# A hybrid decoder block on one core: queries and keys split before their way through DRAM, the identity loaded later, fewer idle products at the start

## The chip, the cores and the metric

The kernel runs on one core of a Trainium2 chip. The metric is the device time of one launch in microseconds; the time quoted is the median of three runs. Beside it stands one profiled execution, whose span runs from the first to the last instruction of the core.

## What is computed

One layer of a decoder block over 512 tokens of width 1024, in float32. The part that the change touches is the attention of the middle stage:

```python
h = h + 0.5 * swiglu(rmsnorm(h, norm_ffn1[i]), ffn1_w1[i], ffn1_w3[i], ffn1_w2[i])
z = rmsnorm(h, norm_mix[i]) @ w_in[i]
q, kc, vc, ksl, vsl, kw, vw, g, u = jnp.split(z, split_at, axis=-1)
...
q = rope(q.reshape(B, L, N_HEADS, HEAD_DIM), pos)
kc = rope(kc.reshape(kvshape), pos)
ksl = rope(ksl.reshape(kvshape), pos)
...
s = jnp.einsum('bqghd,bsgd->bghqs', qc, k_w).astype(jnp.float32) * scale
p_win = masked_softmax(s, wmask)
o_win = jnp.einsum('bghqs,bsgd->bqghd', p_win.astype(v_w.dtype), v_w)
```

There are 8 query heads of width 64, two key heads, and three branches: compressed, selected and window keys. Beside the attention runs a diagonal state space mixer (S5); after both come the output projection, a second SwiGLU, a gated per-layer embedding and a last norm.

## The kernel before

**Products in three parts.** A float32 operand is split in a high part, rounded to the type that TensorE takes in one pass (FR), and the low remainder. A product is the sum of three: high by high, high by low, low by high (`mm3`). The high part is made by ScalarE (a copy or a scaled activation), the low part by VectorE (a subtraction). Weights come from DRAM in units of 128 x 1024 (`load_unit`, L114; split in L159 and L160), through a ring of four raw buffers and three split ones, on SyncE's queue.

**Stages.** By the trace: the first feed-forward network to about 375 us, the mixer to 603 us, the second network to about 975 us, the gate and the last norm to the end. Activations lie transposed, 128 rows of the model by 512 tokens, in eight tiles `h`.

**The start.** SyncE loads the first weight unit in halves, the eight tiles of `h` and three more units. GpSimd loads the identity (L126), makes a bfloat16 copy of it (`identb`, L128) and fills `ones` (L130). TensorE multiplies `ones` by `ones` `WARM` times into a bank that nobody reads (L134, `ps_D<-ones`); each such product in full float32 shows as two records. The real first products, `ps_A` and then `ps_B`, take `xh` (L181, ScalarE) and `xl` (L182, VectorE), which are `h` scaled by the norm's gain and split. The squares for the norm are L187 and L191 (ScalarE) and L192 (VectorE).

**The mixer's queries and keys.** `rotary` (L963) turns two projections: four products and two sums on VectorE give the two rotated halves, which go to DRAM unsplit (L974, L975): keys to `kd`, queries to `qd`. Rows return in another order, so that a head's 64 numbers lie on 64 partitions. For keys, four blocks `kf` are loaded twice (L983, L984), ScalarE makes `KA` (high, in both halves of the partitions) and VectorE makes `KB` (low, in the lower half). For queries, `scores` (L1130) loads for each of the four blocks of 128 tokens two tiles `qf`, twice each (L1142, L1143); ScalarE scales and rounds into `QA` and `QB` (L1144, L1145), VectorE puts the low part into the upper half of `QA` (L1146), and ScalarE clears the upper half of `QB` (L1148).

**The scores.** For each group of heads, TensorE multiplies `QA` by `KA`, `QB` by `KB` and adds the mask (`ps_B` and `ps_C`, two banks each); VectorE takes the row maxima (L1165), ScalarE the exponentials with their sums (L1168). Only then is the bank free. Into the same stretch fall the gated unit of S5 (`glu`, L1093 to L1109) and the compressed keys (L1043 and the products from `raw`).

**What sets the order.** The order of instructions on each engine is written out: `ENGINE_ORDER` holds for each engine the steps from one traced instruction to the next, `TILE_ORDER` pairs of instructions of which the second follows the first, and `impose` turns both into dependencies. An engine runs its list strictly in that order; SyncE's list is the order in which its DMAs are issued.

Of the kernel before, what the change touches and what calls it, by code (L numbers as in the profile page):

```python
# [10 lines left out]
F32 = mybir.dt.float32  # L11
FR = mybir.dt.float32r
BF = mybir.dt.bfloat16
I32 = mybir.dt.int32
AF = mybir.ActivationFunctionType
OP = mybir.AluOpType
# [3 lines left out]
SEQ = 512  # L20
# [56 lines left out]
def block_kernel(ctx: ExitStack, tc: tile.TileContext, a: dict, out: bass.AP):  # L77
    nc = tc.nc
# [47 lines left out]
    nc.gpsimd.dma_start(ident, a["ident"])  # L126
# [669 lines left out]
    qd = dram.tile([2, 128, 2, SEQ], F32, tag="qd", name="qd")  # L796
    kd = dram.tile([128, 2, SEQ], F32, tag="kd", name="kd")
# [3 lines left out]
    def mixer(ctx):  # L801
# [161 lines left out]
        def rotary(dst, tag):  # L963
            oa = proj(tag)
            yield
            ob = proj(tag)
            a1, b1, a2, b2 = (tp.tile([128, SEQ], F32, tag=n, name=n) for n in ("r1", "rb1", "r2", "r3"))
            V.tensor_tensor(a1, oa, cosr, OP.mult)
            V.tensor_tensor(a2, oa, sinr, OP.mult)
            V.tensor_tensor(b1, ob, sinr, OP.mult)  # L970
            V.tensor_tensor(b2, ob, cosr, OP.mult)
            V.tensor_tensor(a1, a1, b1, OP.subtract)
            V.tensor_tensor(a2, a2, b2, OP.add)
            nc.sync.dma_start(dst[:, 0], a1)  # L974
            nc.sync.dma_start(dst[:, 1], a2)  # L975
            yield

        def kq():
            yield from rotary(kd, "A")
            for b in range(4):  # L980
                kf = mp.tile([128, SEQ], F32, tag="ra", name="kf", bufs=2)
                src = kd[32 * b:32 * b + 32].rearrange("r a t -> (r a) t")
                nc.sync.dma_start(kf[0:64], src)  # L983
                nc.sync.dma_start(kf[64:128], src)  # L984
                S.copy(KA[:, b], kf)
                V.tensor_tensor(KB[0:64, b], kf[0:64], KA[0:64, b].bitcast(F32), OP.subtract)
            yield from rotary(qd[0], "B")
# [142 lines left out]
        def scores(qb, env, pool, tags="B", stage=("ra", "ra")):  # L1130
# [5 lines left out]
            for i, (hs, st) in enumerate(zip((slice(0, 4), slice(4, 8)), stage)):  # L1136
                src = qd[i].rearrange("(h r) a t -> (r a) h t", h=4)[:, :, tq]
                if st == "ra":
                    qf = mp.tile([128, 4, 128], F32, tag=st, name="qf", bufs=2)
                else:  # L1140
                    qf = tp.tile([128, 4, 128], F32, tag=st, name="qf")
                nc.sync.dma_start(qf[0:64], src)  # L1142
                nc.sync.dma_start(qf[64:128], src)  # L1143
                S.activation(QA[:, hs], qf, AF.Copy, scale=0.125)  # L1144
                S.activation(QB[0:64, hs], qf[0:64], AF.Copy, scale=0.125)  # L1145
                V.scalar_tensor_tensor(QA[64:128, hs], qf[64:128], 0.125, QA[64:128, hs].bitcast(F32),  # L1146
                                       OP.mult, OP.subtract)
            S.copy(QB[64:128].rearrange("p h q -> p (h q)"), zero[64:128, 0:1].to_broadcast([64, 1024]))  # L1148
# [126 lines left out]
        def chain(*gs):  # L1275
            for g in gs:
                yield from g
# [17 lines left out]
        envs = {qb: {} for qb in range(4)}  # L1295
        s5g, pg, cg, gg = s5_all(), chain(kq(), rotary(qd[1], "B"), cmp_kv(), v_gates()), cmp_all(), glu()
        s3, s2 = scores(3, envs[3], mp, TS, G3), scores(2, envs[2], mp, TS2, G2)
# [106 lines left out]
    with tc.tile_pool(name="gate", bufs=2, reuse_waits="tile") as gp:  # L1404
# [72 lines left out]
G3 = "r1", "r2"  # L1477
G2 = "r3", "ra"
TW, TY, TP, TS, TS2 = "C", "D", "D", "B", "BC"
PROJ = 12  # L1480
WARM = 32
# [351 lines left out]
```

## Time and profile before

| | us |
|---|---|
| median of 3 runs | 1046.07 (1045.25 to 1046.2) |
| the profiled execution | 1045.7 |
| its span | 1043.9 |
| TensorE, share of the span | 98% |
| VectorE, share of the span | 78% |
| ScalarE, share of the span | 51% |

The time lies 1.8 us above the span in the profiled execution. A busy TensorE says little by itself, since the ends of its products are modelled and overlap; what counts is the distance between the starts of its products, and who is named in the chain of work that ended last.

### The profile page before, as it was taken

The page shows a single profiled execution, that of the slowest core. Times are in us where ns is not written, and L with a number is a line of the kernel's source. Part 1 is how long each engine was busy: PE and PEld are TensorE (multiplying, and loading weights), DVE is VectorE, ACT ScalarE, POOL GpSimd, SP SyncE. Part 2 cuts the span into 40 slices and gives each one's busy share as a digit, 9 for nine tenths or more (in the row PEclk, how much of TensorE's full clock was granted, in tenths as well). Part 3 has the DMA queues.
Part 4 walks back from the last instruction along what each step waited for, and adds up shares of the span by engine and source line. Part 5 has one row for each costly group of instructions (what it writes and reads, how often), then busy time and mean ns, then how long its engine had stood idle before and what let it go on. Part 6 is the DMA issues. An engine that isn't in the chain of part 4 may idle for free.

```text
span 1043.9 us, 16750 instructions
## 1 busy us (share of the span) xinstructions
PE 1023.4 (98%) x6386; PEld 897.8 (86%) x6386; DVE 813.1 (78%) x1357; ACT 533.8 (51%) x933; POOL 76.3 (7%) x99
## 2 busy tenths in 40 slices
PE   9999999999999999999999999999999999999995
PEld 8888899889989888896577677998999899899885
DVE  6999997778887777999798988884576477467676
ACT  6354265345425531349879846663354255155453
POOL 1000011001001010000000001101011011000000
PEclk9999999999999999999999999999999999999998
DMA  8536375756745739753710064457265545534222
GB/s 307 111 81 176 73 186 163 226 136 151 206 116 154 271 109 201 241 169 101 242 61 1 21 202 142 119 134 202 61 152 153 150 108 127 169 99 125 89 74 82
DMA packets 73121, 148.52 MB, mean 142 GB/s; under 512 B 19520, under 2 KB 30784, under 8 KB 72784
## 3 DMA queue, kind: packets, MB, share of 16 engines
q1 hardware_dynamic: 60624, 127.05, 39.0%
q0 software_dynamic: 11552, 20.22, 11.9%
q8 instruction: 50, 0.82, 0.3%
q14 instruction: 31, 0.25, 0.1%
q10 hardware_dynamic: 864, 0.17, 0.1%
HBM read 121.96 MB, written 15.73 MB: 132 GB/s over the span
## 4 chain that ended last, share of the span: by engine, by line
PE 94%; DVE 2%; ACT 2%; issue 1%; POOL 0%; DVEq 0%; POOLq 0%; ACTq 0%
PE ps_C L134 28%; PE ps_B L134 25%; PE ps_A L134 24%; PE ps_D L134 16%; ACT ps_B L1168 1%; DVE nmax L1165 1%; PE ps_C L685 0%; DVE lo L160 0%; ACT QB L1148 0%; DVE xn L283 0%; PE ps_D L938 0%; DVE cs L1043 0%; ACT QB L1145 0%; ACT hi L159 0%; ACT QA L1144 0%
## 5 line engine op out<-in xcount | busy, mean ns | idle before, releaser
L159 ACT CAST hi<-raw 128x1024 fp32r<-128x1024 f32 (+2 forms) x206 | 212.4, 1043 | 254.4 <-PE ps_C L134 103.6
L160 DVE TENSOR_TENSOR lo<-raw,hi 128x1024 fp32r<-128x1024 f32 (+2 forms) x206 | 246.7, 1211 | 49.2 <-ACT hi L159 48.6
L134 PE MATMUL ps_C<-hq,hi 128*128 128x512 f32 x704 | 218.5, 391 | 0.0
L134 PEld LDWEIGHTS ps_C<-hq,hi 128*128 128x128 f32 x704 | 127.1, 188 | 23.0 <-issue 0.6
L134 PE MATMUL ps_C<-hq,lo 128*128 128x512 f32 x352 | 137.3, 390 | 0.0
L134 PE MATMUL ps_A<-xh,hi 128*128 128x256 f32 (+1 forms) x432 | 135.0, 313 | 0.0
L134 PE MATMUL ps_A<-xh,lo 128*128 128x256 f32 (+1 forms) x432 | 134.1, 310 | 0.0
L134 PE MATMUL ps_A<-xl,hi 128*128 128x256 f32 (+1 forms) x432 | 134.0, 310 | 0.0
L134 PEld LDWEIGHTS ps_A<-xh,hi 128*128 128x128 f32 x432 | 81.5, 189 | 5.8 <-issue 0.7
L134 PE MATMUL ps_B<-sh,hi 128*128 128x256 f32 x304 | 86.5, 285 | 0.0
L134 PEld LDWEIGHTS ps_A<-xl,hi 128*128 128x128 f32 x432 | 81.6, 189 | 5.7 <-issue 0.5
L134 PE MATMUL ps_B<-sh,lo 128*128 128x256 f32 x304 | 85.3, 281 | 0.5 <-DVE lo L160 0.5
L134 PEld LDWEIGHTS ps_A<-xh,lo 128*128 128x128 f32 x432 | 81.6, 189 | 4.6 <-DVE lo L160 0.2
L134 PE MATMUL ps_B<-sl,hi 128*128 128x256 f32 x304 | 85.4, 281 | 0.0
L487 DVE SCALAR_TENSOR_TENSOR h<-ps_C,h 128x512 f32<-128x512 f32 x64 | 44.1, 689 | 48.4 <-PE ps_C L134 48.3
L134 PEld LDWEIGHTS ps_C<-hq,lo 128*128 128x128 f32 x352 | 66.1, 188 | 14.5 <-DVE lo L160 0.3
L134 PE MATMUL ps_D<-sl,hi 128*128 128x256 f32 x236 | 66.4, 281 | 0.6 <-DVE sl L302 0.6
L134 PE MATMUL ps_D<-sh,lo 128*128 128x256 f32 x236 | 66.4, 281 | 0.0
L134 PE MATMUL ps_D<-sh,hi 128*128 128x256 f32 x236 | 66.3, 281 | 0.0
L363 POOL DMA_DIRECT2D raw<-in_wpack x38 | 35.5, 933 | 412.9 <-DMA raw<-in_wpack 309.2
L369 POOL DMA_DIRECT2D raw<-raw x38 | 32.8, 864 | 391.3 <-DVE lo L160 383.9
L134 PEld LDWEIGHTS ps_B<-sh,hi 128*128 128x128 f32 x304 | 57.2, 188 | 1.0 <-issue 0.2
(405 smaller groups left out, 2328.0 us busy)
## 6 DMA issues: line engine op xcount, KB each, us to landing
raw<-in_wpack SPq DMA_DIRECT2D x171, 512.0 KB, 4.2
raw<-in_wpack POOLq DMA_DIRECT2D x38, 256.0 KB, 4.8
raw<-raw POOLq DMA_DIRECT2D x38, 256.0 KB, 3.3
so<-s5o SPq DMA_DIRECT2D x8, 512.0 KB, 5.4
h<-in_xT SPq DMA_DIRECT2D x8, 256.0 KB, 5.1
s5f<-fs SPq DMA_DIRECT2D x4, 512.0 KB, 3.3
s5o<-gt SPq DMA_DIRECT2D x4, 512.0 KB, 3.7
s5t<-tcs SPq DMA_DIRECT2D x2, 1024.0 KB, 5.8
```

What stands on the lines that cost most here:

```text
L134: return PE.matmul(o, lhsT, rhs, start=start, stop=stop, **kw)
L159: S.copy(hi[:, c], raw[:, c])
L160: V.tensor_tensor(lo[:, c], raw[:, c], hi[:, c].bitcast(F32), OP.subtract)
L363: nc.gpsimd.dma_start(a0[:, 1], src[:, 0:512], accum_op=OP.add)
L369: nc.gpsimd.dma_start(a1[:, 1], a0[:, 1], accum_op=OP.add)
L487: V.scalar_tensor_tensor(h[:, m, :], o, 0.5, h[:, m, :], OP.mult, OP.add)
L1165: V.tensor_reduce(mc, s_, AX.X, OP.max, negate=True)
L1168: S.activation(s_[:, i, r], s_[:, i, r], AF.Exp, bias=mc[:, i, r:r + 1], accum_out=dc[:, i, r:r + 1])
```

## The change

1. `rotary` takes a scale and splits each rotated half before its way through DRAM: ScalarE makes the high part `rh` (L976), VectorE the low part in place, and each is written with a DMA of its own (L977, L980). `qd` and `kd` hold both parts.
2. `KA` and `KB` are loaded ready from `kd` with three DMAs (L986); the copies and subtractions on `kf` go.
3. `QA` and `QB` are loaded ready from `qd` with three DMAs for each block of tokens (L1138); the two activations, the activation for `QB`, the subtraction and the clearing on ScalarE go. GpSimd clears the upper half of `QB` instead (L1136).
4. The identity is loaded on SyncE's queue, at a later place.
5. 20 idle products in place of 32.
6. The tables of orders are new for all engines and through the whole program.

```diff
-    nc.gpsimd.dma_start(ident, a["ident"])
+    nc.sync.dma_start(ident, a["ident"])
...
-    qd = dram.tile([2, 128, 2, SEQ], F32, tag="qd", name="qd")
-    kd = dram.tile([128, 2, SEQ], F32, tag="kd", name="kd")
+    qd = dram.tile([2, 256, 2, SEQ], F32, tag="qd", name="qd")
+    kd = dram.tile([2, 128, 2, SEQ], F32, tag="kd", name="kd")
...
-        def rotary(dst, tag):
+        def rotary(dst, tag, scale):
...
-            nc.sync.dma_start(dst[:, 0], a1)
-            nc.sync.dma_start(dst[:, 1], a2)
+            for i, t in enumerate((a1, a2)):
+                hi = mp.tile([128, SEQ], FR, tag="ra", name="rh", bufs=2)
+                S.activation(hi, t, AF.Copy, scale=scale)
+                nc.sync.dma_start(dst[0, :, i], hi.bitcast(F32))
+                lo = t.bitcast(FR)
+                V.scalar_tensor_tensor(lo, t, scale, hi.bitcast(F32), OP.mult, OP.subtract)
+                nc.sync.dma_start(dst[1, :, i], t)
...
-            yield from rotary(kd, "A")
-            for b in range(4):
-                kf = mp.tile([128, SEQ], F32, tag="ra", name="kf", bufs=2)
-                src = kd[32 * b:32 * b + 32].rearrange("r a t -> (r a) t")
-                nc.sync.dma_start(kf[0:64], src)
-                nc.sync.dma_start(kf[64:128], src)
-                S.copy(KA[:, b], kf)
-                V.tensor_tensor(KB[0:64, b], kf[0:64], KA[0:64, b].bitcast(F32), OP.subtract)
-            yield from rotary(qd[0], "B")
+            yield from rotary(kd, "A", 1.0)
+            for part, dst in ((0, KA[0:64]), (0, KA[64:128]), (1, KB[0:64])):
+                nc.sync.dma_start(dst.bitcast(F32), kd[part].rearrange("(b r) a t -> (r a) b t", b=4))
+            yield from rotary(qd[:, 0:128], "B", 0.125)
...
-            for i, (hs, st) in enumerate(zip((slice(0, 4), slice(4, 8)), stage)):
...
-                nc.sync.dma_start(qf[0:64], src)
-                nc.sync.dma_start(qf[64:128], src)
-                S.activation(QA[:, hs], qf, AF.Copy, scale=0.125)
-                S.activation(QB[0:64, hs], qf[0:64], AF.Copy, scale=0.125)
-                V.scalar_tensor_tensor(QA[64:128, hs], qf[64:128], 0.125, QA[64:128, hs].bitcast(F32),
-                                       OP.mult, OP.subtract)
-            S.copy(QB[64:128].rearrange("p h q -> p (h q)"), zero[64:128, 0:1].to_broadcast([64, 1024]))
+            G.memset(QB[64:128].rearrange("p h q -> p (h q)").bitcast(F32), 0.0)
+            for part, dst in ((0, QA[0:64]), (0, QB[0:64]), (1, QA[64:128])):
+                nc.sync.dma_start(dst.bitcast(F32), qd[part].rearrange("(h r) a t -> (r a) h t", h=8)[:, :, tq])
...
-WARM = 32
+WARM = 20
...
-        "21:23 54 -55:7 48:3 -51:2 49:32 37:3 -40:12 49:3 -52:4 24:3 21:6 -27:9 53:3 -83 26:3 53:3 -41:3 38:3 "
+        "21:14 51 -52 51:9 -60 59:14 -73:2 71:2 -73:2 71:19 28:3 -31:3 28:3 18:3 -52:4 48:9 -30:9 21:3 -51 79:6 "
```

**The start, TensorE.** Before, the idle products `ps_D<-ones` stand thus among the first products of the first weight unit:

```order
L134 MATMUL ps_D<-ones 128x128 x23
L134 MATMUL ps_A<-xh,hi 128x512
L134 MATMUL ps_D<-ones 128x128 x7
L134 MATMUL ps_A<-xl,hi 128x512
L134 MATMUL ps_A<-xh,lo 128x512
```

Now:

```order
L134 MATMUL ps_D<-ones 128x128 x14
L134 MATMUL ps_A<-xh,hi 128x512
L134 MATMUL ps_D<-ones 128x128
L134 MATMUL ps_A<-xl,hi 128x512
L134 MATMUL ps_A<-xh,lo 128x512
```

Ahead of the second real product stand 15 idle ones where 30 stood. Of the other five, one stands between later products of `ps_A`, two ahead of the first product of `ps_B` and two before its third.

**The start, ScalarE.** Behind the split of the first half of weight unit 0, before (`acc` and `xn` are squares for the norm):

```order
L159 CAST hi<-raw 128x512
L187 ACTIVATE acc<-h 128x512
L181 ACTIVATE xh<-h,gains 128x512
L191 ACTIVATE xn<-h 128x512
L181 ACTIVATE xh<-h,gains 128x512 x5
L159 CAST hi<-raw 128x512
L181 ACTIVATE xh<-h,gains 128x512
L191 ACTIVATE xn<-h 128x512
L181 ACTIVATE xh<-h,gains 128x512
L159 CAST hi<-raw 128x1024
```

and now:

```order
L159 CAST hi<-raw 128x512
L181 ACTIVATE xh<-h,gains 128x512 x3
L159 CAST hi<-raw 128x512
L181 ACTIVATE xh<-h,gains 128x512 x5
L187 ACTIVATE acc<-h 128x512
L191 ACTIVATE xn<-h 128x512
L159 CAST hi<-raw 128x1024
```

The squares have moved behind all eight `xh`, and the second half of weight unit 0 is split after three of them instead of after six. VectorE's list has moved in the same way: all eight `xl` and the low part of that half stand ahead of the first sum of squares.

**The first scores, ScalarE.** Where the scores of the last two blocks of tokens begin, beside the gated unit (`gt`, `oh`, `sg`), before:

```order
L857 ACTIVATE gt<-gt 128x512
L1144 ACTIVATE QA<-qf 128x512
L1145 ACTIVATE QB<-qf 64x512
L1093 CAST oh<-yt 128x512
L1144 ACTIVATE QA<-qf 128x512 x2
L1148 CAST QB<-zero 64x1024
L1145 ACTIVATE QB<-qf 64x512
L1106 ACTIVATE sg<-ps_A,bglu 128x512
L1168 ACTIVATE ps_B,den<-ps_B,nmax 128x512 x2
L1145 ACTIVATE QB<-qf 64x512
L1144 ACTIVATE QA<-qf 128x512
L1145 ACTIVATE QB<-qf 64x512
```

and now, where the exponentials stand in L1158:

```order
L855 ACTIVATE gt<-yt 128x512
L1158 ACTIVATE ps_B,den<-ps_B,nmax 128x512
L1158 ACTIVATE ps_C,den<-ps_C,nmax 128x384
L857 ACTIVATE gt<-gt 128x512
L1158 ACTIVATE ps_C,den<-ps_C,nmax 128x384
L1093 CAST oh<-yt 128x512
L1158 ACTIVATE ps_B,den<-ps_B,nmax 128x512
L1106 ACTIVATE sg<-ps_A,bglu 128x512
L1158 ACTIVATE ps_B,den<-ps_B,nmax 128x512
```

No query is prepared here any more, and the first exponentials come ahead of the gated unit's last steps instead of behind them.

**The way through DRAM, SyncE.** The queue where the last rotated queries (`qd<-r`) leave, before:

```order
L974 DMA qd<-r_4578 128x512
L114 DMA raw<-in_wpack 128x1024
L901 DMA so<-s5o 128x1024 x2
L1000 DMA kcd<-ra 64x512
L1142 DMA qf<-qd 64x4x128
L975 DMA qd<-r_4580 128x512
L1143 DMA qf<-qd 64x4x128
```

and now, with the high parts in `rh`:

```order
L980 DMA qd<-r_4565 128x512
L977 DMA qd<-rh 128x512
L114 DMA raw<-in_wpack 128x1024
L901 DMA so<-s5o 128x1024
L980 DMA qd<-r_4567 128x512
L1138 DMA QB<-qd 64x8x128 x2
L1000 DMA kcd<-ra 64x512 x2
L114 DMA raw<-in_wpack 128x1024
L1138 DMA QA<-qd 64x8x128
```

There are two writes for each rotated half, and the loads of queries stand behind the last of them, since one load now takes all eight heads.

More of the change, by code (lines that the diff above doesn't have):

```diff
@@ L1128, in mixer, with scores @@
         den = mp.tile([128, 4, 3, 8], F32, name="den")
-        def scores(qb, env, pool, tags="B", stage=("ra", "ra")):
+        def scores(qb, env, pool, tags="B"):
             nk = (qb + 1) * 128
@@ L1135, in scores @@
             QB = pool.tile([128, 8, 128], FR, tag="QB", name="QB", bufs=2)
-            for i, (hs, st) in enumerate(zip((slice(0, 4), slice(4, 8)), stage)):
[L1137 to L1141, printed above, removed]
-                nc.sync.dma_start(qf[0:64], src)
-                nc.sync.dma_start(qf[64:128], src)
-                S.activation(QA[:, hs], qf, AF.Copy, scale=0.125)
-                S.activation(QB[0:64, hs], qf[0:64], AF.Copy, scale=0.125)
-                V.scalar_tensor_tensor(QA[64:128, hs], qf[64:128], 0.125, QA[64:128, hs].bitcast(F32),
-                                       OP.mult, OP.subtract)
-            S.copy(QB[64:128].rearrange("p h q -> p (h q)"), zero[64:128, 0:1].to_broadcast([64, 1024]))
+            G.memset(QB[64:128].rearrange("p h q -> p (h q)").bitcast(F32), 0.0)
+            for part, dst in ((0, QA[0:64]), (0, QB[0:64]), (1, QA[64:128])):
+                nc.sync.dma_start(dst.bitcast(F32), qd[part].rearrange("(h r) a t -> (r a) h t", h=8)[:, :, tq])
             env.update(QA=QA, QB=QB)
@@ L1295, in mixer @@
         envs = {qb: {} for qb in range(4)}
-        s5g, pg, cg, gg = s5_all(), chain(kq(), rotary(qd[1], "B"), cmp_kv(), v_gates()), cmp_all(), glu()
-        s3, s2 = scores(3, envs[3], mp, TS, G3), scores(2, envs[2], mp, TS2, G2)
+        s5g, pg, cg, gg = s5_all(), chain(kq(), rotary(qd[:, 128:256], "B", 0.125), cmp_kv(), v_gates()), cmp_all(), glu()
+        s3, s2 = scores(3, envs[3], mp, TS), scores(2, envs[2], mp, TS2)
         drain(s5_input())
@@ L1476 @@
 ORDER = 3, 2
-G3 = "r1", "r2"
-G2 = "r3", "ra"
 TW, TY, TP, TS, TS2 = "C", "D", "D", "B", "BC"
 PROJ = 12
-WARM = 32
+WARM = 20
 S1 = 32
```

320 rows, old and new, of tables (ENGINE_ORDER, TILE_ORDER) are left out of this document.

## The prediction

> **What bounds the kernel now.** First the page: the busy times and the chain that ended last.
>
> ```profile
> PE 1023.4 (98%) x6386; PEld 897.8 (86%) x6386; DVE 813.1 (78%) x1357; ACT 533.8 (51%) x933; POOL 76.3 (7%) x99
> PE 94%; DVE 2%; ACT 2%; issue 1%; POOL 0%; DVEq 0%; POOLq 0%; ACTq 0%
> ```
>
> TensorE carries 94% of the chain, so most of the program can only shrink by fewer products, and the change removes none but idle ones. What can go is the 6% on other engines (some 60 us) and the useless products at the start. So I asked next where these lie: busy times by stretch (columns PE, PEld, DVE, ACT, POOL, granted clock, DMA share, GB/s), and the chain inside the stretch of the scores.
>
> ```profile
> 400.00:476.00 76.00, 75.34 (x495) 65.14 (x494) 72.04 (x155) 29.08 (x51) 0.00 (x0) 1.00 0.71 203
> 476.00:524.00 48.00, 44.97 (x252) 28.85 (x251) 40.78 (x73) 42.85 (x104) 0.00 (x0) 1.00 0.56 166
> 524.00:603.00 79.00, 78.73 (x375) 58.62 (x374) 73.86 (x160) 68.90 (x172) 0.00 (x0) 1.00 0.09 30
> ...
> 477.69:497.33 19.64, 18.16 (x86) 11.71 (x84) 18.75 (x32) 18.44 (x44) 0.00 (x0) 1.00 0.23 68
> 497.33:516.00 18.67, 17.12 (x108) 9.46 (x108) 13.59 (x24) 16.72 (x43) 0.00 (x0) 1.00 0.83 251
> ...
> by line: PE ps_A L134 17.8%; ACT ps_B L1168 17.6%; DVE nmax L1165 14.4%; PE ps_B L134 12.7%; issue 6.3%; ACT QB L1148 5.2%; DVE cs L1043 4.5%; ACT QB L1145 4.2%; ACT QA L1144 3.9%; ACT sg L1106 3.2%; DVE ol L1109 3.0%; ACT ps_C L1168 2.5%;
> PEld ps_B L134 <- ACT ps_B L1168: 4.9, 9, 1.2
> ```
>
> From 476 to 524 us ScalarE is busy for 42.85 of 48 us, and weight loading for 28.85, the lowest of the three mixer stretches in share. The fourth and fifth rows cut the dense part of it in two. The last two rows are the chain of the 40 us from 476 to 516, and the longest wait of TensorE in the stretch: it waits nine times for an exponential before it may reuse a bank. TensorE holds little more than 30% of this piece of the chain; the scores are paced by maximum and exponential on VectorE and ScalarE, and between them, on the chain, stand the three lines that the change deletes: 5.2 + 4.2 + 3.9 = 13.3% of 40 us, which is **5.3 us**.
>
> The start, from the order of time (start, length, then what):
>
> ```profile
> 2.37 7.34 PE L134 MATMUL ps_D<-ones 128*128 128x128 f32 x46 [2.37 <-POOL ones L130]
> 9.46 0.48 PE L134 MATMUL ps_A<-xh,hi 128*128 128x512 f32 x1
> 9.78 1.72 PE L134 MATMUL ps_D<-ones 128*128 128x128 f32 x14
> ...
> 16.82 0.39 PE L134 MATMUL ps_A<-xh,lo 128*128 128x512 f32 x1
> 17.05 0.39 PE L134 MATMUL ps_B<-xh,hi 128*128 128x512 f32 x1
> ...
> 1.32 0.77 POOL L126 DMA_DIRECT2D ident<-in_ident  x1 [0.37 <-issue]
> 6.00 0.29 POOL L128 CAST identb<-ident 128x128 bf16<-128x128 f32 x1 [3.67 <-DMA ident<-in_ident]
> 6.17 0.63 ACT L191 ACTIVATE xn<-h 128x512 f32<-128x512 f32 x1 [0.69 <-DMA h<-in_xT]
> 12.36 1.03 ACT L159 CAST hi<-raw 128x1024 fp32r<-128x1024 f32 x1
> 13.95 1.22 DVE L160 TENSOR_TENSOR lo<-raw,hi 128x1024 fp32r<-128x1024 f32 x1
> ```
>
> Products of 512 columns start 0.23 us apart (16.82 to 17.05). All 24 of `ps_A` are issued by 17.05; laid end to end they would have begun at 17.05 - 24 x 0.227 = 11.6 us. This "dense start" is the measure of the head: what it gains is how much earlier the dense start lies.
>
> **The change part by part: the start.** What the first products wait for:
>
> ```profile
> L119 SPq DMA_DIRECT2D h<-in_xT x8: 421/432/631, 1.2 to 5.2; - x8
> L181 ACT ACTIVATE xh<-h,gains x8: 707/714/725, 4.8 to 11.7; 128x512 fp32r<-128x512 f32 x8
> L182 DVE SCALAR_TENSOR_TENSOR xl<-h,gains,xh x8: 747/748/749, 7.4 to 12.7; 128x512 fp32r<-128x512 f32 x8
> ...
> DMA to landing us min/median/max: 3.0/5.1/5.6
> ...
> L114 SPq DMA_DIRECT2D raw<-in_wpack x1: 328/328/328, 6.2 to 6.2; - x1
> ...
> DMA to landing us min/median/max: 5.9/5.9/5.9
> ```
>
> The first tile of `h` lands at 1.2 + 3.0 = 4.2 us, the last at 5.2 + 5.6 = 10.8, weight unit 1 at 6.2 + 5.9 = 12.1. ScalarE waits for the second tile until 6.17, so 1.9 us lie between tiles one and two, and (10.8 - 6.15) / 7 = 0.66 us between the seven pieces of the same size behind. In the wide gap the identity lands (`identb` waits for it until 6.00). Moved behind, it frees between 0 and 1.9 - 0.66 = 1.2 us; I take the middle, 0.6.
>
> Step by step: last tile of `h` at 10.2; its `xh` 0.71 later, 10.9; VectorE makes eight `xl` (8 x 0.748) and a half of `lo` (0.69) from about 5.5, so the last `xl` is there at 12.1, and `ps_A` ends near 12.6. TensorE itself: 14 idle products are 28 records, 19 slow and 9 fast by the next two rows, so they end at 2.37 + 4.10 + 9 x 0.103 = 7.4, and 24 products with two idle ones fill the time to 13.3. Unit 1 is there at 11.5, ScalarE comes to it behind `acc` and `xn` (2 x 0.63) at 12.4 and is done at 13.4; VectorE's `lo`, 1.22, at 14.65. Then stands the third product of `ps_B`, with 26 behind it, and from there nothing waits. Dense start 14.65 - 26 x 0.227 = 8.75. Gain 11.6 - 8.75 = **2.9 us**. If the identity frees nothing, all is 0.6 later, 2.3; if it frees all, 3.5. The cover of what has moved: the squares now end on ScalarE near 10.9 + 8 x 0.63 + 2 x 1.05 = 18 us, and the first norm needs them only after the two weight units, 48 products or 10.9 us, that stand between. The identity lands near 16 us (an estimate: 5.2 MB of loads ahead of it at the 384 GB/s of the second row below, from 2.4 us); GpSimd's `identb` waits for it and, behind it on GpSimd, the first norm's power, whose squares are later still. Without that cover the cost is the lateness itself.
>
> ```profile
> 2.37:6.47 4.10, 4.10 (x19) 4.10 (x20) 0.69 (x1) 2.24 (x5) 0.29 (x1) 1.00 0.94 322
> 6.47:9.46 2.99, 2.99 (x29) 2.99 (x29) 2.62 (x5) 2.92 (x5) 0.00 (x0) 1.00 1.04 384
> ```
>
> These are the idle products: 19 records in the first 4.10 us (0.216 each), 29 in the next 2.99 (0.103). The array runs at half pace until 6.47. The Trainium skill, "TensorE: Matmul & The Clock Gate", Part 1 (the HAM clock gate), says that the clock is released by about 3.4 us of sustained activity in a window that runs freely, so the moment differs from run to run; by it, 14 idle products (5 us) could end before the release. The trace agrees on the size: 4.1 us from the first product. Its result is a rival below.
>
> **The queries.** Deleted and added, from the groups:
>
> ```profile
> L1146 DVE SCALAR_TENSOR_TENSOR QA<-qf,QA 64x512 fp32r<-64x512 f32 x8 | 5.4, 689 | 0.2
> L1145 ACT ACTIVATE QB<-qf 64x512 fp32r<-64x512 f32 x8 | 5.0, 622 | 0.0
> L1144 ACT ACTIVATE QA<-qf 128x512 fp32r<-128x512 f32 x8 | 4.9, 622 | 0.0
> L1148 ACT CAST QB<-zero 64x1024 fp32r<-64x1024 f32 x4 | 4.2, 1043 | 0.1
> L986 DVE TENSOR_TENSOR KB<-kf,KA 64x512 fp32r<-64x512 f32 x4 | 2.7, 678 | 0.0
> L985 ACT CAST KA<-kf 128x512 fp32r<-128x512 f32 x4 | 2.5, 617 | 6.8 <-DMA kf<-kd 6.8
> ```
>
> ScalarE loses 5.0 + 4.9 + 4.2 + 2.5 = 16.6 us and gains six activations of 128x512 at 0.622, 3.7. VectorE loses 5.4 + 2.7 = 8.1 and gains six of the form of L182, 6 x 0.748 = 4.5. The additions fall between 400 and 460 us, where ScalarE idles and VectorE does not (72.04 of 76).
>
> The chain would give 5.3 us. What is late next? From 477.69 to 497.33 ScalarE falls from 18.44 by 4.8 (one L1148, six of the others), but VectorE only from 18.75 by three L1146, to 16.7: it becomes the bound, so at most 19.64 - 16.7 = 2.9 us go. From 497.33 to 516 both fall to 12.2 (ScalarE by two L1148 and four others, VectorE by two L1146); there TensorE decides, with 17.12 busy by modelled ends, and I take 2.0 of its waits of 4.9 us in the stretch. Sum 4.9. Against it: between 400 and 476 VectorE has 4.5 more and 2.7 less, +1.8 at 95% busy; it has 4 us of slack, so I charge 0.7 of it. Net **4.2 us**; bounds 0 (the whole wait returns as a wait for maxima) and 7.5 (the 4.9 of banks go, too).
>
> **GpSimd's clearing** replaces L1148. Its price is not in the trace; the nearest row and the power behind it:
>
> ```profile
> L130 POOL MEMSET ones<- 128x128 f32 x1 | 0.2, 237 | 0.0
> 377.44 1.04 POOL L325 TENSOR_TENSOR ri<-ms,negh 128x4 f32<-128x4 f32 x1 [3.08 <-DVE ms L324]
> ```
>
> Eight times the columns: at most 8 x 0.237 = 1.9 us, at least 0.24; I take 1.9. Two stand ahead of the mixer norm's power, which waits 3.08 us for its input: of 3.8 us at most 0.7 stick out. Without that cover it costs up to 3.8, and the norm's row `rb` and the scaled rope tables wait behind the power. I take 0.
>
> **The DMAs.** Issues, KB each, us to landing, and the stretch where they fall:
>
> ```profile
> qf<-qd SPq DMA_DIRECT2D x16, 128.0 KB, 3.8
> kf<-kd SPq DMA_DIRECT2D x8, 128.0 KB, 5.0
> qd<-r SPq DMA_DIRECT2D x4, 256.0 KB, 3.8
> ...
> 404.00:460.00 56.00, 56.00 (x358) 48.31 (x357) 53.14 (x117) 16.45 (x29) 0.00 (x0) 1.00 0.84 241
> ```
>
> Written: queries 4 x 256 KB become 8, keys 2 become 4: +1.5 MB. Read: 16 x 128 KB become 12 x 256, 8 x 128 become 3 x 512: +1.5 MB. So some 3 MB more, most of it where the DMA engines are 84% busy at 241 GB/s. At 241 / 0.84 = 287 GB/s of a busy engine set they take 10.5 us of DMA time, and 0.16 x 56 = 9.0 are free, with ten nearly idle us behind. Barely hidden: 0, with up to 10.5 if not. On SyncE's queue the first load of queries stands behind the last write, and weights and `kcd` behind it; that wait is one landing, 3.8 us.
>
> **The new orders** elsewhere move no work; nothing in the rows of other stretches says that they gain or lose. I take 0, give or take 1.5.
>
> Sum: 1043.9 - 2.9 - 4.2 = 1036.8 of span. The profiled execution took 1045.7, 1.8 over its span, and the median is 1046.07; the same sum on the median is 1046.07 - 7.1 = **1039.0 us**.
>
> **The rivals.**
> 1. *The scores stay paced by maxima and exponentials.* Each bank still passes VectorE and ScalarE in turn, and products were only waiting for that. For it: 14.4% and 17.6% of the chain are L1165 and L1168. Against it: ScalarE had deleted lines between them. Then only the head gains: 1043.2.
> 2. *The clock is released late.* Up to 3.4 us of real products at half pace, 1.7 us lost: head 1.2, time 1040.7. For it: the slow rows above. Against it: the arrival of data, not the pace, ends the head until 13 us.
> 3. *Nothing is left*: the scores as in 1, and the head's gain is given back to VectorE, whose work behind the head has no slack:
>
> ```profile
> 25.00:125.00 100.00, 99.98 (x531) 85.54 (x530) 97.98 (x209) 40.20 (x57) 7.18 (x8) 1.00 0.45 112
> ```
>
> VectorE is busy for 97.98 of these 100 us. For it: that share. Against it: much of it prepares S5, which the mixer needs 300 us later. Near 1045.5.
> 4. *Slower: the DMA engines.* The 3 MB delay weights or S5 tables in 404 to 460, TensorE stands, and it decides once more than 9.2 us are lost there (7.1 + 2.1). All 10.5 us on the path give 1039.0 + 10.5 = 1049.5. For it: 84% busy. Against it: that average has gaps, and 460 to 470 is free.
> 5. *More*: orders close waits in other stretches as well: near 1035.
>
> **How the numbers follow.** Forecast 0.52 (1036 to 1042), more 0.06, late clock 0.05, scores only paced 0.13, nothing left 0.10, DMA 0.14. A measurement of this kernel tells 0.2% from no change, 2.1 us: faster is below 1044.0 (0.52 + 0.06 + 0.05 + 0.11 = 0.74), slower above 1048.2 (0.14), the rest 0.12. The range leaves out the slower case and the end of the faster one: 1034.5 to 1046.5.
>
> **What would show it.** Right: real products from 7.5 us, the first dense ones of `ps_B` near 14.65; waits of TensorE for L1158 below 3 us in the scores; ScalarE below 32 of 48 us there. Wrong: TensorE waiting for `raw` or S5 tables between 400 and 470; VectorE's maxima as the longest part of the chain; the power on GpSimd later than its sum; half-pace real products behind 7.5 us.

## The result, and the profile after

The changed kernel takes 1037.68 us, the median of four runs (1036.99 to 1037.96), against 1045.88 for four runs of the kernel before beside it: a ratio of 0.9921, 95% interval 0.9904 to 0.9938, or 8.3 us of 1046 (6.5 to 10.0). A second measurement, `after_again` below, gave the same ratio. The forecast was 7.1 us. The profiled execution took 1037.4, 1.8 over its span of 1035.6.

The page of the changed kernel, busy times and the chain that ended last:

```profile
PE 1020.9 (99%) x6362; PEld 896.4 (87%) x6362; DVE 810.4 (78%) x1351; ACT 523.5 (51%) x915; POOL 80.9 (8%) x102
PE 93%; DVE 3%; issue 1%; ACT 1%; DMA 0%; POOL 0%; SPq 0%; DVEq 0%; POOLq 0%; ACTq 0%
```

TensorE lost 2.5 us of busy time (12 idle products, 24 records), and ScalarE 10.3. The shares hardly move; such a change is read from its stretches. Busy times by stretch of the changed kernel (columns as before: PE, PEld, DVE, ACT, POOL, granted clock, DMA share, GB/s), then the chain and TensorE's waits for exponentials within the scores, which now run from 467 to 516:

```profile
476.00:524.00 48.00, 47.73 (x273) 32.89 (x272) 39.88 (x81) 34.37 (x92) 0.00 (x0) 1.00 0.57 159
467.00:516.00 49.00, 48.73 (x289) 32.94 (x287) 40.53 (x73) 37.11 (x95) 1.84 (x2) 1.00 0.68 182
404.00:460.00 56.00, 56.00 (x361) 47.82 (x360) 52.45 (x116) 18.73 (x33) 0.00 (x0) 1.00 0.91 257
```

```profile
by line: PE ps_A L134 49.9%; PE ps_B L134 33.7%; PE ps_C L134 6.9%; PE ps_D L134 5.2%; ACT ps_B L1158 1.4%; PE ps_D L938 1.3%; DVE nmax L1155 1.2%; PE ps_C L1067 0.4%; issue 0.3%; ACTq L1158 0.0%
```

```profile
PEld ps_B L134 <- ACT ps_B L1158: 2.2, 7, 0.4
PE ps_B L134 <- ACT ps_B L1158: 0.2, 1, 0.2
```

The first row is that of the weight loads, which the profile lists apart from the products; the row of before in the prediction (4.9 us, nine times) is of the same kind. The products' own waits of before, between 476 and 524:

```profile
PE ps_B L134 <- ACT ps_B L1168: 2.8, 5, 1.1
```

TensorE, which held little more than 30% of the chain from 476 to 516, now holds 97% of the one from 467 to 516. Its weight loads wait 2.2 us for exponentials instead of 4.9, and its products 0.2 instead of 2.8. In the order of time the first product with the mask has moved from 478.34 to 467.57, 10.8 us, more than anything else; 4.1 of that are the lead with which the mixer begins. The loads of `QA` and `QB` for the first two blocks of tokens have all landed by 465.95, before the values are all projected, so the scores are mixed with those products and with the gated unit instead of following them. That makes the scores themselves longer, not shorter: from the first product with the mask to that of the 32nd block they take 43.8 us instead of 37.3. What shrinks is TensorE's idle time. From the mixer norm's diagonal to the last product of the output projection it was busy for 239.1 of 243.5 us, and now for 238.3 of 238.8: the gaps fell from 4.4 to 0.5 us.

The head of the changed kernel in order of time (start, length, what):

```profile
7.15 0.50 PE L134 MATMUL ps_A<-xh,hi 128*128 128x512 f32 x1
...
11.43 0.62 ACT L187 ACTIVATE acc<-h 128x512 f32<-128x512 f32 x1
11.95 0.62 ACT L191 ACTIVATE xn<-h 128x512 f32<-128x512 f32 x1
12.47 1.03 ACT L159 CAST hi<-raw 128x1024 fp32r<-128x1024 f32 x1
...
13.00 0.39 PE L134 MATMUL ps_A<-xh,lo 128*128 128x512 f32 x1
...
13.54 1.23 DVE L160 TENSOR_TENSOR lo<-raw,hi 128x1024 fp32r<-128x1024 f32 x1 [0.24 <-ACT hi L159]
...
14.82 0.50 PE L134 MATMUL ps_B<-xh,lo 128*128 128x512 f32 x1
```

The real products begin at 7.15 (forecast 7.5) and the third product of `ps_B` at 14.82 (14.65). The 24th product of `ps_B`, by which the two heads can be compared once all is dense, starts at 20.43 instead of 22.94, 2.5 us earlier.

Where the lead arises, from the starts of the same instruction in both traces:

| instruction on TensorE | before | after | lead |
|---|---|---|---|
| 24th product of `ps_B` | 22.94 | 20.43 | 2.5 |
| first transposed product of the first feed-forward layer | 126.06 | 123.27 | 2.8 |
| mixer norm, sum of squares | 376.20 | 372.76 | 3.4 |
| mixer norm, diagonal (`dg`) | 381.87 | 377.74 | 4.1 |
| last score of the first 32 blocks | 515.63 | 511.38 | 4.3 |
| last value product | 602.23 | 594.41 | 7.8 |
| output projection, last | 625.35 | 616.52 | 8.8 |
| end of the span | 1043.90 | 1035.58 | 8.3 |

Some 4.1 us were there when the mixer's products began, 4.7 came in the mixer, and 0.5 went again behind it. The mixer's 4.7 show only behind the first scores: at the last of the 32 blocks the lead is 4.3, because other products now stand among them. These are single executions. In the second one of the changed kernel, `after_again`, the lead grows by 2.9 in the mixer, for a reason given under the DMA engines.

### The profile page after: what moved, and what is told of

It is laid out like the page before. It is cut to its first block, busy times and chain, and to the rows that moved or that the text cites. A ratio compares the mean times of both kernels' runs of the same rounds, so it can differ in the third digit from the quotient of the medians.

```text
span 1035.6 us, 16669 instructions
## 1 busy us (share of the span) xinstructions
PE 1020.9 (99%) x6362; PEld 896.4 (87%) x6362; DVE 810.4 (78%) x1351; ACT 523.5 (51%) x915; POOL 80.9 (8%) x102
## 4 chain that ended last, share of the span: by engine, by line
PE 93%; DVE 3%; issue 1%; ACT 1%; DMA 0%; POOL 0%; SPq 0%; DVEq 0%; POOLq 0%; ACTq 0%
PE ps_C L134 28%; PE ps_B L134 25%; PE ps_A L134 25%; PE ps_D L134 15%; DVE lo L160 1%; DMA h<-in_xT 0%; DVE xn L229 0%; PE ps_C L685 0%; ACT xh L181 0%; POOL ri L325 0%; DVE acc L192 0%; DVE xn L283 0%; PE ps_D L938 0%; ACT hi L159 0%; DVE ple L1449 0%
```

## The experiments

Gains are given as the ratio to the kernel before, times 1046 us, with the interval; one interval is some 1.3 us to either side, so that a difference below 1 us between two of them is decided by the traces or not at all.

| kernel | ratio (interval) | us against before |
|---|---|---|
| `h_ident` | 0.9988 (0.9980 to 0.9997) | -1.3 (-2.1 to -0.3) |
| `h_head` | 0.9982 (0.9973 to 0.9991) | -1.9 (-2.8 to -0.9) |
| `h_ffn1` | 0.9966 (0.9954 to 0.9979) | -3.6 (-4.8 to -2.2) |
| `m_mix` | 0.9955 (0.9942 to 0.9969) | -4.7 (-6.1 to -3.2) |
| `b_clear` | 0.9995 (0.9986 to 1.0003) | -0.5 (-1.5 to +0.3) |
| `after_again` | 0.9921 (0.9908 to 0.9935) | -8.3 (-9.6 to -6.8) |
| `a_idle32` | 0.9938 (0.9925 to 0.9950) | -6.5 (-7.8 to -5.2) |
| `a_halves` | 0.9918 (0.9905 to 0.9932) | -8.6 (-9.9 to -7.1) |
| `a_sdose` | 0.9935 (0.9923 to 0.9948) | -6.8 (-8.1 to -5.4) |
| `a_vdose` | 0.9925 (0.9913 to 0.9938) | -7.8 (-9.1 to -6.5) |
| `a_dma` | 0.9948 (0.9935 to 0.9960) | -5.4 (-6.8 to -4.2) |
| `a_klate` | 0.9926 (0.9914 to 0.9939) | -7.7 (-9.0 to -6.4) |

**The start, in four kernels.** The kernel before with the identity alone:

```
-    nc.gpsimd.dma_start(ident, a["ident"])
+    nc.sync.dma_start(ident, a["ident"])
```

> The kernel before with one edit: SyncE loads the identity (behind the S5 tables) instead of GpSimd. Theory of the prediction: the identity stood among the tiles of h and delayed them by 0.6 us, so h lands 0.6 earlier and the time falls by up to 0.6, to about 1045.3. Rival 1: it delayed nothing; what it held was GpSimd, which fills `ones` behind it, so the idle products of TensorE begin at 1.2 us instead of 2.4, the clock is released earlier, and the first real product starts up to 1.2 us earlier: down to 1044.7, with h landing as before. Rival 2: neither counts, 1045.9.

It gained 1.3 us, more than the 0.6 of the landing theory. In its trace the last tile of `h` lands at 10.50 against 10.79, 0.3 earlier; in the changed kernel it lands at 10.78, and in two of the kernels below, with the same queue, at 10.54 and 10.99. So the landing is worth 0.3 at most, which is within the spread, and nothing where it counted. `ones` is filled earlier: the idle products start at 1.15 instead of 2.37. The first rival is the nearer one. Its profiled execution (1045.5, one of the slowest of eleven) does not show the full gain, since there the clock was released only at 7.3 us and the first real product began at 9.25 against 9.46; so what the early start is worth seems to change from one execution to the next. That the 1.3 us come by `ones` rests on the expectation and on the earlier start; no trace here shows them in full.

The kernel before with the whole changed head, all engines in the changed order up to about 25 us:

```
-WARM = 32
+WARM = 20
-    nc.gpsimd.dma_start(ident, a["ident"])
+    nc.sync.dma_start(ident, a["ident"])
```

> The kernel before with the head of the changed one: identity on SyncE, 20 idle products, and the changed orders on all engines up to about 25 us (the first 87 products of TensorE); behind that the orders of before, and the queries as before. Theory: the head is worth 2.5 to 2.9 us and keeps it to the end, 1043.0 to 1043.4. Rival: the lead is given back to waits behind the head, since those orders were made for the later start: 1045 or more.

It gained 1.9: less than the theory, more than the rival. Its `ps_B` ends where that of the changed kernel does (24th product at 20.41), 2.5 us early, but at the first transposed product 1.2 are left. The wait that takes them, from TensorE's waits between 15 and 35 us; the changed kernel has none there:

```profile
PE ps_D L134 <- DVE exi L543: 1.0, 1, 1.0
```

At 28 us TensorE stands before the product of the first norm's diagonal, behind VectorE, which does S5 preparation (`exi`) between the steps of the norm. The old order has its other products ready elsewhere. So the next kernel took the changed orders on to the mixer's norm, still with the old queries:

> The kernel before with the head and, unlike h_head, all the changed orders up to the mixer's norm (the whole first feed-forward layer and the S5 tables beside it); from the norm on the old orders and the old queries. The head alone gave 2.1 us and the mixer alone 4.3, 6.4 together, against 8.3 to 8.5 for the whole change. Theory: the missing 2 us lie in the order of the first feed-forward layer, which is made for the earlier start: 3.5 to 4.2 us in all, 1041.8 to 1042.5. Rival: they come only where both parts meet (each needs the other, or the orders of the last layer): 1044.

3.6 us, as the theory said, and no wait there. The order of the first feed-forward layer is worth the difference, 1.7 us by the ratios and 1.5 by the traces at 123 us (the head of this execution was 0.5 later).

The changed kernel with the old count of idle products:

```
-WARM = 20
+WARM = 32
```

> The changed kernel with 12 more idle products at its start (32, as before). Theory: 24 more records run at 0.103 us behind the release of the clock, the real products begin near 9.6 us instead of 7.2, and the dense products of ps_B near 15.8 instead of 14.4 (the two ahead of the wait for unit 1 included): 1.0 to 1.5 us slower, 1038.7 to 1039.2. Rival: the count of idle products is without effect, since the arrival of data sets the first products; then 1037.7, and the head's gain is all in the order of squares and casts.

1.8 us of the gain go; the real products begin at 8.74 and `ps_B`'s third product at 16.04, 1.2 later. The count matters: the first tile of `xl` is there at 5.9 us, and the idle products still run for 2.9 us.

The changed kernel with unit 1 split in halves, and the six idle products among the real ones gone:

```
-        return split(raw, (slice(0, 512), slice(512, w)) if i == 0 else (slice(0, w),), keep)
+        return split(raw, (slice(0, 512), slice(512, w)) if i < 2 else (slice(0, w),), keep)
-WARM = 20
+WARM = 14
```

> The changed kernel with weight unit 1 split into hi and lo in two halves, both ahead of the first square on ScalarE and ahead of the first sum of squares on VectorE, and without the six idle products that stand among the real ones. Theory: the wait of ps_B's third product (until 14.82 in the changed kernel) is for the last part of unit 1's lo; with halves it is there by 13.3, and with nothing idle between, ps_B follows ps_A without a gap: 1.1 us faster, 1036.6. Rival: the squares come 0.5 to 1 us later, and the first norm or the second pair of weight units takes the lead back: 1037.7 or slower.

The rival. The step itself worked, the third product of `ps_B` starts at 13.24 instead of 14.82; then TensorE waits for the sum of squares, where it did not before:

```profile
PE ps_D L134 <- DVE acc L192: 1.4, 1, 1.4
```

The sum of squares is complete at 22 us in both kernels: VectorE has eight `xl`, the low parts of four units and seven sums to do by then. It, not the first products, is the end of the changed head, and this version is no better than the changed kernel (0.3 us by the ratios).

**The mixer alone**: the kernel before up to the mixer's norm and from the second half of the output projection on, the changed mixer between.

> The kernel before up to the mixer's norm (32 idle products, identity on GpSimd, the old orders) and again from the second half of the output projection on, with the changed queries and the changed orders of the mixer in between. Theory: the mixer alone is worth what the trace shows between the first S5 product (4.2 us early) and the output projection (8.8 early), 4.0 to 4.7 us: 1041.3 to 1042. Rival: the mixer's gain hangs on the earlier start and the new orders around it, and alone it is 2 or less: 1044 or more.

4.7 us (3.2 to 6.1), the theory. With `h_ffn1` it makes 8.3, the whole change: the two parts add up, and the orders of the last layer are worth nothing that shows. Its profiled execution has a wait of 1.5 us for S5, and its lead grows by 3.3 between the mixer's norm and the output projection; in the changed kernel it grew by 4.7 without that wait and by 2.9 with it.

**Which engine paces the scores.** The old kernel with GpSimd clearing `QB`:

```
-            S.copy(QB[64:128].rearrange("p h q -> p (h q)"), zero[64:128, 0:1].to_broadcast([64, 1024]))
+            G.memset(QB[64:128].rearrange("p h q -> p (h q)").bitcast(F32), 0.0)
```

> The kernel before with one part of the change: GpSimd instead of ScalarE clears the lower half of QB, four times; all other orders as before. Three of the four (1.04 us each) stood on ScalarE among the scores. Theory: ScalarE paces the old scores, and 1.5 to 3 us go: 1043 to 1044.5. Rival: maxima on VectorE or the arrival of queries pace them as well, and nothing goes: 1046.

3.1 us less on ScalarE among the old scores bring 0.5, and the interval includes no gain at all; in the trace the 32nd block starts 0.6 earlier relative to the start of the mixer. Next, idle work on ScalarE, and on VectorE, among the scores of the changed kernel:

```
                 V.tensor_reduce(mc, s_, AX.X, OP.max, negate=True)
+                if qb > 1 and j % 4 == 2:
+                    for _ in range(3):
+                        S.copy(dose, zero[:, 0:1].to_broadcast([128, 64]))
```

> The changed kernel with idle work on ScalarE in the scores: ahead of the exponential of every fourth of the first 32 blocks three small activations of 128x64, 24 in all, some 0.2 us each, about 5 us between 467 and 516 us, where ScalarE is busy for 37 of 49. Theory: the scores are bound by TensorE now (48.7 of 49 busy), and ScalarE has room: within 0.5 us of the changed kernel. Rival: ScalarE still paces the scores, as it did before, and the time rises by 3 to 5 us, to 1041 or more.

```
                 V.tensor_reduce(mc, s_, AX.X, OP.max, negate=True)
+                if qb > 1 and j % 4 == 2:
+                    V.tensor_reduce(dose[:, 0:1], zero[:, 0:1].to_broadcast([128, SEQ]), AX.X, OP.max)
```

> The changed kernel with idle work on VectorE in the scores: behind the maximum of every fourth of the first 32 blocks a reduction of 512 columns, 8 in all, some 0.6 us each, about 5 us between 467 and 516 us, where VectorE is busy for 40.5 of 49. The prediction's step: VectorE is the bound that takes ScalarE's place, then 2.5 to 5 us slower, 1040 to 1043. Rival: TensorE is the bound and VectorE has room: within 0.7 us of the changed kernel.

The kernel with the load on ScalarE: the added work in the groups between 460 and 520 us (busy, mean ns), and the busy times of the scores:

```profile
L1160 ACT COPY dose<-zero 128x64 f32<-128x64 f32 x24 | 5.8, 241 | 0.5
```

```profile
467.00:516.00 49.00, 47.63 (x276) 31.83 (x275) 38.88 (x69) 40.41 (x118) 1.84 (x2) 1.00 0.67 177
```

The same two views of the kernel with the load on VectorE:

```profile
L1159 DVE TENSOR_REDUCE dose<-zero 128x1 f32<-128x512 f32 x8 | 5.4, 677 | 0.0
```

```profile
467.00:516.00 49.00, 48.34 (x278) 32.28 (x276) 43.74 (x78) 37.30 (x94) 1.84 (x2) 1.00 0.64 176
```

5.8 us on ScalarE cost 1.5 by the ratios. From the first product with the mask to that of the 32nd block the trace has 45.6 us, against 43.8 in the changed kernel: 1.8. 5.4 us on VectorE cost 0.4 by the ratios, and the same distance grows by 0.5, to 44.3. The ratios alone hardly tell the two loads apart, their intervals overlap; the distance does, since in four other profiled executions with the changed scores (`after_again`, `m_mix`, `a_dma`, `a_klate`) it is 43.79 to 43.82. TensorE's products wait 1.3 us for exponentials with the load on ScalarE, 0.5 with the one on VectorE, and 0.2 without. Neither expectation for ScalarE holds as it stands: it is not the bound, but a quarter of what it is given comes out. The prediction's step on VectorE falls: with 43.7 of 49 us busy it still is not what TensorE waits for.

**The DMA engines.** Every write of rotated queries and keys made twice, 3 MB more:

```
                 nc.sync.dma_start(dst[0, :, i], hi.bitcast(F32))
+                nc.sync.dma_start(xd[next(extra)], hi.bitcast(F32))
...
                 nc.sync.dma_start(dst[1, :, i], t)
+                nc.sync.dma_start(xd[next(extra)], t)
```

> The changed kernel with each of its twelve writes of rotated keys and queries made twice, the second to memory that nobody reads: 3 MB more between 408 and 455 us, where the DMA engines are busy for 91% at 257 GB/s (282 GB/s of a busy set: 10.6 us of their time, against 5 free in the 56 us). Theory: what is late then are weights and S5 tables that were early, 0 to 1 us. Rival (the prediction's fourth): the DMA engines are full there, and 3 to 10 us are lost, 1041 to 1048.

2.8 us slower than the changed kernel: nearer to the rival. Beside it the changed kernel ran a second time:

> The changed kernel itself, beside the three that add one load to it each: 1037.5 to 1038.3.

TensorE's longest wait between 425 and 470 us, first in this second execution of the changed kernel, then in the one with doubled writes, and the windows of the latter:

```profile
PE ps_D L134 <- DVE z L920: 1.5, 1, 1.5
```

```profile
PE ps_D L134 <- DVE z L922: 2.2, 1, 2.2
```

```profile
444.00:448.00 4.00, 4.00 (x23) 3.44 (x21) 3.96 (x11) 0.96 (x2) 0.00 (x0) 1.00 1.07 330
448.00:452.00 4.00, 2.72 (x28) 2.10 (x26) 3.86 (x8) 1.76 (x3) 0.00 (x0) 1.00 0.89 330
452.00:456.00 4.00, 2.94 (x16) 2.61 (x17) 3.91 (x7) 1.69 (x5) 0.00 (x0) 0.58 0.92 335
456.00:460.00 4.00, 4.00 (x21) 4.00 (x20) 3.16 (x9) 0.30 (x1) 0.00 (x0) 0.57 0.99 256
460.00:464.00 4.00, 4.00 (x32) 3.86 (x30) 2.77 (x7) 1.66 (x4) 0.00 (x0) 1.00 1.02 278
```

The profiled execution with doubled writes is the slowest of its five (1038.8 to 1042.5) and the only one with a mean granted clock of 0.991 (the others 0.994 to 0.996). Its first product with the mask comes 5.3 us later than in the first execution of the changed kernel. The wait makes 2.2 of that; the products behind it, from 453.1 to 459.5, run at half pace, which makes some 3.2 more. So this trace shows a worse case than the 2.8 us.

The changed kernel itself is at the edge: in its first profiled execution there is no such wait (span 1035.6), in this second one 1.5 us (1037.1). What is late are S5 tables. SyncE's loads of keys in the first execution (duration of the issue in ns, place; then us to landing), and VectorE's wait for a table in the first and in the second execution:

```profile
L986 SPq DMA_DIRECT2D KA<-kd x2: 644/656/668, 415.3 to 417.8; - x2
L986 SPq DMA_DIRECT2D KB<-kd x1: 591/591/591, 416.0 to 416.0; - x1
...
DMA to landing us min/median/max: 7.4/9.4/13.7
```

```profile
DVE t L907 <- DMA ti<-s5t: 2.0, 1, 2.0
```

```profile
DVE t L907 <- DMA ti<-s5t: 3.8, 1, 3.8
```

The three loads of keys, 512 KB each, land 7 to 14 us after their issue (the 128 KB of before: 5.0), and one of the tables behind them, 256 KB, takes 12.3 in the first execution. So they were moved on SyncE's list, behind the last table:

```
 ti<-s5t
-KA<-kd
-KB<-kd
 raw<-in_wpack
 so<-s5o
-KA<-kd
...
 so<-s5o
+KA<-kd
+KB<-kd
 qd<-rh
 raw<-in_wpack
+KA<-kd
```

> The changed kernel with the three loads of keys (KA twice, KB; 512 KB each) moved on SyncE from 415 to 418 us, where the loads behind them take 10 to 14 us to land, to 439 to 443, where the DMA engines have 30% free; the keys are needed from 467 on. Theory: the added DMA traffic costs the changed kernel up to 1.5 us in some of its executions (S5 tables land late, VectorE waits for them, TensorE for VectorE near 451 us), and this goes: 1036.5 to 1037.2. Rival: the loads now delay the queries as much: 1037.5 or more.

The rival, about. TensorE's waits between 396 and 560 us:

```profile
PE ps_B L134 <- DMA QA<-qd: 1.0, 1, 1.0
PE ps_D L134 <- DVE z L920: 0.7, 1, 0.7
```

The wait for S5 is 0.7, half of that in the second execution, and one for the queries stands beside it. Moving these three loads to this place frees nothing; whether another order would is not shown.

Not tried: the new queries in the old order of the mixer. There the compressed keys use the two `ra` buffers ahead of the last rotation, which now needs them. Not tried either: the old queries in a new order. In the kernel before, two of the four tiles of raw queries for the first scores had landed by 461.4 and a third by 472.6. ScalarE, busy for 29 of the 76 us from 400 to 476, splits the first of them at 476.04, where the old order has it, and does not wait for a load there. So how much of the mixer's 4.7 us is the split ahead of DRAM, and how much a new order alone could have had, is open.

## Why the prediction held, step by step

- **The head, 2.9.** Its own lead is 2.5 to the 24th product of `ps_B`, but alone it brought 1.9 (`h_head`): the first norm took 1.0 back. Within it the identity was mis-sized: 0.6 for the landing of `h`, measured 0 in the changed kernel and 0.3 in `h_ident`. What it did bring lies in the start of `ones`, a wait that the prediction had in a row (`ps_D<-ones`, released by `ones` on GpSimd) and did not use. The wait for `lo` of unit 1 set the time, as forecast, but that its 14.65 was right to 0.2 is luck: the last `xh` ends at 11.52 and not at 10.9, while the two squares behind it, for which the prediction has 1.5 us (10.9 to 12.4), start 0.52 apart, so that the cast of unit 1 starts at 12.47 all the same.
- **The clock's late release** (rival 2) was there, and harmless: in the first execution only 7 of the 28 idle records ran between 4.94 and 6.05, at half pace, against 11 in the second (rows in the last section), and both have `ps_B`'s third product at 14.8 and 14.6.
- **Queries and scores, 4.2.** Measured 4.7 (3.2 to 6.1) by `m_mix`. The size is right, the mechanism in part, and so the nearness of 4.2 to 4.7 is partly luck. That the deleted lines cost time on the chain is borne out by a trace (0.6 us for the clearing alone, `b_clear`). The step that VectorE becomes the bound from 477.69 to 497.33 is wrong: TensorE is the bound, with gaps of 0.5 us where 4.4 stood, and the scores lie earlier and among other products, which the prediction did not consider. Its 4.9 us of waits, of which it took 2.0, are those of weight loads; the products' own were 2.8. Of ScalarE's relief the loads show the price: 0.16 (`b_clear`, 0.5 of 3.1, with an interval that reaches zero) to 0.26 (`a_sdose`, 1.5 of 5.8) of each microsecond; for the 13 that left the scores (5.0 + 4.9 + 3 x 1.04) that is 2.1 to 3.4 us of the 4.7, if a load put on the changed kernel tells what a relief of the old one is worth. That the rest is the earlier start is argued from the trace and not shown by itself.
- **The signs.** Waits for L1158 below 3 us: 2.2 by the weight loads, 0.2 by the products. ScalarE below 32 of 48 us between 476 and 524: 34.37, missed. Now 34 exponentials and four weight casts lie in that window instead of 32 and three, and its instructions overlap less: their lengths fell by 11.1 us, the busy time by 8.5.
- **GpSimd's clearing**, priced at 1.9 with 0.24 and 1.9 as ends, takes 0.954 each, and the pair ahead of the mixer's norm ends at 368.8, 5 us before GpSimd's power for that norm (L325): nothing on the path, as forecast.

```profile
L1136 POOL MEMSET QB<- 64x1024 f32 x4 | 3.7, 954 | 96.6 <-PE ps_D L134 94.6 <-issue 2.0
```

- **DMA, 0 with up to 10.5.** "Barely hidden" was right: 0 in one execution, 1.5 in another, 2.8 for 3 MB more.
- **The new orders, 0 give or take 1.5.** This term was mis-sized: 1.7 by the ratios (`h_ffn1` less `h_head`, each to about a microsecond) and 1.5 by the traces in the first feed-forward layer, at the edge of its bounds. The account of the runs is 1.9 + 1.7 + 4.7 = 8.3 against 2.9 + 0 + 4.2 = 7.1: the head 1.0 less, the orders 1.7 more, the mixer 0.5 more. That the first two errors go in opposite directions is luck. The prediction found that nothing in the rows of other stretches says that they gain or lose; the wait in question is not in the trace of before; it arises when the head gets earlier and the order does not follow.

## What to carry to other kernels

When work in front of a hand-written order gets faster, the order behind it has to be made for the new time, or the first place where two engines meet takes the lead back: here 1.0 of 2.5 us. Work that is taken off a half-busy engine is not worth its length: put a known load there and on its neighbour, and the two slopes (here 0.26 for ScalarE and 0.07 for VectorE by the ratios, 0.31 and 0.09 by the traces) tell which one counts and how much. And a stage whose inputs lie ready early can be mixed with other products, so ask of a change not only what it deletes but what it lets start.

## What the runs showed of the hardware

**The clock's release.** Records of idle products in two executions of the changed kernel, by stretch; first the one with the late release, then the other:

```profile
1.16:4.94 3.78, 3.78 (x17) 3.78 (x18) 0.69 (x1) 2.37 (x3) 0.00 (x0) 1.00 0.80 236
4.94:6.05 1.11, 1.11 (x7) 1.11 (x7) 0.75 (x1) 0.25 (x1) 0.00 (x0) 1.00 0.99 356
```

```profile
1.16:4.94 3.78, 3.78 (x17) 3.78 (x18) 0.69 (x1) 2.37 (x3) 0.00 (x0) 1.00 0.78 250
4.94:6.05 1.11, 1.11 (x11) 1.11 (x11) 0.75 (x1) 0.36 (x2) 0.00 (x0) 1.00 1.07 378
```

The same program runs at half pace until 7.4 us in one execution and until 4.9 in the other, 3.8 to 6.2 us after its first product (0.21 us from record to record before, 0.11 or less behind), while the column of the granted clock says 1.00 in both. The Trainium skill, "TensorE: Matmul & The Clock Gate", Part 1, gives a window of about 3.4 us and a transition around 4 us, half a microsecond to either side by where the window stands; these two traces have 3.8 and 6.2.

**The clock falls again.** In the windows of `a_dma` above, TensorE waits 2.2 us from 450.9 on, and from 452 to 460 the mean granted clock is 0.58 and 0.57; until 459.3 products of 280 columns start 0.23 us apart, and 0.13 behind that. The wait of 1.5 us in the second execution of the changed kernel did not do it. The same page of the Trainium skill, in its section on HAM oscillation, sets the limit for gaps at about 3.4 us; in this one execution 2.2 sufficed, in a stretch of small products that TensorE did not fill either.

**Landing times.** In the profiled execution of `a_vdose` the fourth tile of `h` landed at 9.71 us instead of 8.14, with the same issue, and the whole head was 1.6 us later. In eight profiled executions with the changed head the 24th product of `ps_B` starts between 20.12 and 22.02. So a single profile of a start like this is good to 1 or 2 us, the first row of the table of leads included.
